# Gating each half of the scan branch's projection at once, and adding it to the other branch in DRAM by adding transfers

## The chip, the cores and the metric

The kernel runs on one core of one Trainium2 chip. Its engines are TensorE (PE in the profile; its weight loads are a row of their own, PEld), VectorE (DVE), ScalarE (ACT), GpSimd (POOL) and SyncE (SP). Each works through its own instructions in order and waits on the others by semaphores. Transfers between DRAM and on-chip memory are issued by an engine (rows marked SPq and ACTq: issued by SP or by ACT) and carried out by 16 DMA engines. The metric is the device time of one execution, in microseconds (us).

## The reference, cut to what matters

One residual block for 512 positions of width 2048. Two branches are computed from one input projection, a retention branch (`y_r`, width 2048) and a scan branch (`y_s`, width 4096). What the change touches is how they are merged:

```python
y_s = rmsnorm((y_s * silu(z)), ssd_norm_w)
p_r = einsum('bse,ed->bsd', y_r, w_br_ret)      # 2048 -> 2048
p_s = einsum('bse,ed->bsd', y_s, w_br_ssd)      # 4096 -> 2048
merged = sigmoid(gate_r) * p_r + sigmoid(gate_s) * p_s
x = x + einsum('bsd,de->bse', merged, w_out)    # 2048 -> 2048
return rmsnorm(x, norm_f_w)
```

The inner dimension of `p_s` is twice that of `p_r`, and the kernel computes it in two halves. The scale of `y_s`'s norm is one number per position, so the kernel applies it after the projection, together with the gate.

## The kernel before, in words

All activations are kept transposed: channels on the 128 partitions, 512 positions along a row. A projection has three parts:

- `load_operands` (L192) brings 8 operand tiles `r` of 256 rows into on-chip memory and prepares them (`first_half`, L168 to L175, on DVE and ACT). `second_halves` (L177 to L185) prepares the other operands (`b`) that the units 1 to 6 need.
- `unit` (L249) computes 256 output rows. There are 8 units in a projection of 2048 outputs. Units 0 and 7 are plain (96 matmuls of 512 columns), units 1 to 6 use a scheme of seven products (168 matmuls of 256 columns). For each of 8 inner steps the weights are loaded by SP (`wf`, L227; 3 buffers), combined by DVE (L230 to L233), split into a high part `whi` (ACT, L148) and a low part `wlo` (DVE, L149), and multiplied by PE (L213 to L215). At the end ACT and DVE collect the sums into a tile `o` (2 buffers, L261 to L270), whose two halves are the 128 x 512 outputs `x`.
- The loop around it does something with each `x`.

Four projections stand behind each other at the end, and this text names them so:

- the **retention projection** (L696 to L704): each output is multiplied by its gate `gr_d` and stored to `m_d` in DRAM;
- the **first scan half** (L709 to L715), over rows 0 to 2047 of `ys_d`: each output is stored as it is to `ps_d`;
- the **second scan half** (L716 to L731), over rows 2048 to 4095: for each output SP loads the partial result `ps_d`, the gate `gs_d` and the other branch `m_d`; POOL multiplies the gate by the norm's scale `R2` (L726); DVE adds the partial result (L727), multiplies by the gate (L728) and adds the other branch (L729); ACT stores to `mm_d` (L731). For unit 7 the result stays on chip as the last operand tile;
- the **output projection** (from L732): its operands are the seven tiles of `mm_d` and the last one.

The tiles that the loops around `unit` load are called `f` and share 4 buffers (L689 to L694). The program is put in order by a scheduler that simulates it, and weight loads have a higher priority than the rest. So SP's queue is one row of weight loads (L227), loads of `f` (L693) and of operands (L197), in an order fixed when the program is built; one that waits holds up all that stand behind it.

## Time and profile before

| what | value |
|---|---|
| time, median of 3 runs (lowest to highest) | 2768.85 us (2766.91 to 2770.41) |
| the profiled execution: its own time / its span | 2769.07 us / 2767.2 us |
| TensorE busy | 2699.1 us (98% of the span) |
| VectorE busy | 2371.0 us (86%) |
| ScalarE busy | 1343.0 us (49%) |
| GpSimd busy | 175.2 us (6%) |
| DMA | 362.46 MB, mean 131 GB/s |

The own time of the profiled execution lies 1.87 us above its span and 0.22 us above the median of the runs. TensorE is the engine that sets the length nearly everywhere; the four projections at the end take up the last fifth, from about 2050 us. Times below are microseconds from the start of the span.

### The profile page before, as it was taken

The page shows a single profiled execution, that of the slowest core. Times are in us where ns is not written, and L with a number is a line of the kernel's source. Part 1 is how long each engine was busy: PE and PEld are TensorE (multiplying, and loading weights), DVE is VectorE, ACT ScalarE, POOL GpSimd, SP SyncE. Part 2 cuts the span into 40 slices and gives each one's busy share as a digit, 9 for nine tenths or more (in the row PEclk, how much of TensorE's full clock was granted, in tenths as well). Part 3 has the DMA queues.
Part 4 walks back from the last instruction along what each step waited for, and adds up shares of the span by engine and source line. Part 5 has one row for each costly group of instructions (what it writes and reads, how often), then busy time and mean ns, then how long its engine had stood idle before and what let it go on. Part 6 is the DMA issues. An engine that isn't in the chain of part 4 may idle for free.

```text
span 2767.2 us, 51984 instructions
## 1 busy us (share of the span) xinstructions
PE 2699.1 (98%) x20448; PEld 2567.6 (93%) x20448; DVE 2371.0 (86%) x3799; ACT 1343.0 (49%) x1923; POOL 175.2 (6%) x130
## 2 busy tenths in 40 slices
PE   6999999999999999999999999999999999999998
PEld 3799999999999999999999999999999989899898
DVE  8788888888878898898989888898889798898997
ACT  4334333343336555566565556556564353433453
POOL 0000000000000100000000000000000000011221
PEclk8999999999999999999999999999999999999999
DMA  4233333333333434343443434344464544557634
GB/s 141 77 96 92 115 100 107 96 100 103 104 112 107 141 108 127 121 129 121 128 142 120 136 108 128 116 132 126 131 200 144 192 155 141 179 169 230 203 123 138
DMA packets 339766, 362.46 MB, mean 131 GB/s; under 512 B 25152, under 2 KB 297792, under 8 KB 339520
## 3 DMA queue, kind: packets, MB, share of 16 engines
q1 hardware_dynamic: 319136, 325.05, 38.2%
q10 hardware_dynamic: 20384, 34.09, 3.3%
q8 instruction: 160, 2.62, 0.4%
q14 instruction: 86, 0.70, 0.1%
HBM read 321.56 MB, written 37.49 MB: 130 GB/s over the span
## 4 chain that ended last, share of the span: by engine, by line
PE 75%; DVE 11%; DMA 8%; issue 3%; ACT 1%; SPq 1%; POOL 0%; DVEq 0%; ACTq 0%; POOLq 0%
PE pb L215 21%; PE pb L214 21%; PE pb L213 20%; DVE wlo L149 3%; DMA wf<-in_w_in_dram 3%; DMA wf<-in_w_br_ssd_dram 2%; PE att L215 2%; PE att L214 2%; PE att L213 2%; PE att L549 1%; PE att L534 1%; DVE wf L230 1%; PE att L666 1%; PE pb L118 1%; PE att L670 1%
## 5 line engine op out<-in xcount | busy, mean ns | idle before, releaser
L148 ACT CAST whi<-wf 128x896 fp32r<-128x896 f32 (+1 forms) x968 | 818.5, 884 | 925.8 <-PE pb L214 390.0
L149 DVE TENSOR_TENSOR wlo<-wf,whi 128x896 fp32r<-128x896 f32 (+1 forms) x968 | 989.9, 1034 | 64.4 <-ACT whi L148 33.3
L213 PE MATMUL pb<-a,whi 128*128 128x256 f32 (+1 forms) x3328 | 1001.8, 304 | 13.7 <-ACT a L118 9.4
L214 PE MATMUL pb<-a,whi 128*128 128x256 f32 (+1 forms) x3328 | 1002.4, 302 | 8.7 <-DVE a L118 8.7
L215 PE MATMUL pb<-a,wlo 128*128 128x256 f32 (+1 forms) x3328 | 999.6, 302 | 5.9 <-DVE wlo L149 5.9
L213 PEld LDWEIGHTS pb<-a,whi 128*128 128x128 f32 x3328 | 636.7, 192 | 41.5 <-ACT a L118 13.3
L214 PEld LDWEIGHTS pb<-a,whi 128*128 128x128 f32 x3328 | 639.1, 192 | 33.9 <-DVE a L118 12.8
L215 PEld LDWEIGHTS pb<-a,wlo 128*128 128x128 f32 x3328 | 637.9, 192 | 29.9 <-DVE wlo L149 7.7
L213 PE MATMUL pb<-b,whi 128*128 128x256 f32 x2112 | 599.6, 284 | 0.0
L215 PE MATMUL pb<-b,wlo 128*128 128x256 f32 x2112 | 598.8, 284 | 0.0
L214 PE MATMUL pb<-b,whi 128*128 128x256 f32 x2112 | 598.0, 284 | 0.0
L230 DVE TENSOR_TENSOR wf<-wf 128x512 f32<-128x512 f32 x400 | 286.2, 715 | 185.3 <-DMA wf<-in_w_in_dram 138.7
L214 PEld LDWEIGHTS pb<-b,whi 128*128 128x128 f32 x2112 | 405.4, 192 | 0.1
L215 PEld LDWEIGHTS pb<-b,wlo 128*128 128x128 f32 x2112 | 405.3, 192 | 0.2
L213 PEld LDWEIGHTS pb<-b,whi 128*128 128x128 f32 x2112 | 405.4, 192 | 0.0
L233 DVE TENSOR_TENSOR wf<-wf 128x256 f32<-128x256 f32 x400 | 175.5, 439 | 3.4
L232 DVE TENSOR_TENSOR wf<-wf 128x256 f32<-128x256 f32 x400 | 174.5, 436 | 3.6
L215 PE MATMUL att<-a,wlo 128*128 128x256 f32 (+1 forms) x480 | 144.6, 306 | 5.3 <-DVE wlo L149 5.3
L213 PE MATMUL att<-a,whi 128*128 128x256 f32 (+1 forms) x480 | 145.5, 305 | 0.0
L214 PE MATMUL att<-a,whi 128*128 128x256 f32 (+1 forms) x480 | 145.3, 305 | 0.0
L215 PEld LDWEIGHTS att<-a,wlo 128*128 128x128 f32 x480 | 91.0, 192 | 10.3 <-DVE wlo L149 6.5
L659 ACT ACTIVATE L<-L,sst 128x128 f32<-128x128 f32 x256 | 78.5, 390 | 35.8 <-DMA L<-A_d 35.8
(221 smaller groups left out, 2736.6 us busy)
## 6 DMA issues: line engine op xcount, KB each, us to landing
wf<-in_w_in_dram SPq DMA_DIRECT2D x640, 256.0 KB, 3.1
wf<-in_w_br_ssd_dram SPq DMA_DIRECT2D x128, 256.0 KB, 3.4
wf<-in_w_out_dram SPq DMA_DIRECT2D x72, 256.0 KB, 3.2
wf<-in_w_in_dram SPq DMA_DIRECT2D x128, 128.0 KB, 2.6
L<-A_d SPq DMA_DIRECT2D x32, 512.0 KB, 3.7
wf<-in_w_br_ret_dram SPq DMA_DIRECT2D x64, 256.0 KB, 3.4
ys_d<-B ACTq DMA_DIRECT2D x32, 256.0 KB, 2.1
r<-ys_d SPq DMA_DIRECT2D x16, 512.0 KB, 6.1
```

The lines of the kernel that those rows point to most:

```text
L118: ins = getattr(self.engine, name)(*args, **kw).ins
L148: ACT.copy(dst_hi, src)
L149: DVE.tensor_tensor(dst_lo, src, dst_hi.bitcast(F32), op=ALU.subtract)
L213: PE.matmul(o, wh, xh, start=b not in started, stop=False, skip_group_check=True)
L214: PE.matmul(o, wh, xl, start=False, stop=False, skip_group_check=True)
L215: PE.matmul(o, wl, xh, start=False, stop=(k == NP - 1), skip_group_check=True)
L230: DVE.tensor_tensor(f2[:, :, 4:6, :], f2[:, :, 1:3, :], f2[:, :, 0:1, :].to_broadcast([P, 2, 2, P]), op=ALU.subtract)
L232: DVE.tensor_tensor(f2[:, :, 0, :], f2[:, :, 2, :], f2[:, :, 4, :], op=ALU.add)
L233: DVE.tensor_tensor(f2[:, :, 6, :], f2[:, :, 3, :], f2[:, :, 0, :], op=ALU.subtract)
L534: PE.matmul(ps[:, :n], k[:, i, sb * P:(sb + 1) * P], q[:, i, sb * P:], start=(i == 0), stop=(i == 1))
L549: PE.matmul(ps[:, :DK], pt[sb][:, (lb - sb) * P:(lb - sb + 1) * P], v[:, sb, :], start=(sb == 0), stop=(sb == lb))
L659: ACT.activation(L[:, i, c, :], L[:, i, c, :], AF.Relu, scale=-1.0, bias=At[:, c, h0 + i:h0 + i + 1])
```

## The change

Each half of the scan branch's projection is now gated as soon as it is computed. In the first scan half SP loads the gate, POOL multiplies it by the norm's scale, ACT stores the scaled gate to a new DRAM array `ss_d`, DVE multiplies the output by it in place (in `o`), and POOL issues a transfer from `o` to `m_d` that adds to what is there. The second scan half loads the scaled gate, multiplies, and adds to `m_d` in the same way; for unit 7 it loads `m_d` and adds on chip. The output projection reads its operands from `m_d`. The arrays `ps_d` and `mm_d` are gone. The text calls the new transfers "adding transfers". Line numbers after the change are up to 3 higher from here on, and 1 lower ahead of it.

```diff
-    ps_d = dp.tile([D, T], F32, name="ps_d")
+    ss_d = dp.tile([D, T], F32, name="ss_d")
     m_d = dp.tile([D, T], F32, name="m_d")
-    mm_d = dp.tile([D, T], F32, name="mm_d")
...
             for e, x in enumerate(unit([w_s[:D, i * 256:(i + 1) * 256]], i % 2, i in PLAIN2)):
                 j = 2 * i + e
-                ACT.dma_start(out=ps_d[j * P:(j + 1) * P, :], in_=x)
+                s = rtile(gs_d, j)
+                POOL.tensor_tensor(s, s, R2, op=ALU.mult)
+                ACT.dma_start(out=ss_d[j * P:(j + 1) * P, :], in_=s)
+                DVE.tensor_tensor(x, x, s, op=ALU.mult)
+                POOL.dma_start(out=m_d[j * P:(j + 1) * P, :], in_=x, accum_op=ALU.add)
         load_operands(ys_d[D:, :])
...
             for e, x in enumerate(unit([w_s[D:, i * 256:(i + 1) * 256]], i % 2, i in PLAIN2)):
                 j = 2 * i + e
-                p = rtile(ps_d, j, last[:, e, :] if i == NP - 1 else None)
-                s, m = rtile(gs_d, j), rtile(m_d, j)
-                POOL.tensor_tensor(s, s, R2, op=ALU.mult)
-                DVE.tensor_tensor(p, p, x, op=ALU.add)
-                DVE.tensor_tensor(p, p, s, op=ALU.mult)
-                DVE.tensor_tensor(p, p, m, op=ALU.add)
+                s = rtile(ss_d, j)
                 if i < NP - 1:
-                    ACT.dma_start(out=mm_d[j * P:(j + 1) * P, :], in_=p)
-        load_operands(mm_d, NP - 1)
+                    DVE.tensor_tensor(x, x, s, op=ALU.mult)
+                    POOL.dma_start(out=m_d[j * P:(j + 1) * P, :], in_=x, accum_op=ALU.add)
+                else:
+                    m = rtile(m_d, j)
+                    DVE.tensor_tensor(s, s, x, op=ALU.mult)
+                    DVE.tensor_tensor(last[:, e, :], s, m, op=ALU.add)
+        load_operands(m_d, NP - 1)
```

SP's queue in the middle of the second scan half, before (`f` tiles are the small loads, `wf` the weights):

```order
L693 DMA f_27273<-gs_d_85 128x512
L693 DMA f_27275<-m_d_87 128x512
L693 DMA f_27282<-ps_d_86 128x512
L227 DMA wf_27553<-in_w_br_ssd_dram 128x2x256 x2
L227 DMA wf_27609<-in_w_br_ssd_dram 128x2x256 x2
L693 DMA f_27284<-gs_d_85 128x512
L227 DMA wf_27665<-in_w_br_ssd_dram 128x2x256 x2
L693 DMA f_27286<-m_d_87 128x512
L693 DMA f_27527<-ps_d_86 128x512
L693 DMA f_27529<-gs_d_85 128x512
L227 DMA wf_27700<-in_w_br_ssd_dram 128x2x256 x2
L693 DMA f_27531<-m_d_87 128x512
```

So the queue before alternates between the two kinds. The same queue at the same place after the change:

```order
L692 DMA f_27578<-ss_d_86 128x512
L692 DMA f_27582<-ss_d_86 128x512
L227 DMA wf_27460<-in_w_br_ssd_dram 128x2x256 x2
L227 DMA wf_27495<-in_w_br_ssd_dram 128x2x256 x2
L227 DMA wf_27590<-in_w_br_ssd_dram 128x2x256 x2
L227 DMA wf_27646<-in_w_br_ssd_dram 128x2x256 x2
L692 DMA f_27820<-ss_d_86 128x512
L692 DMA f_27824<-ss_d_86 128x512
```

Before, six loads of `f` for a unit stand singly between its eight weight loads; after, two stand together ahead of eight weight loads.

POOL's queue at the start of the first scan half after the change (there was nothing there before; `m_d` rows are the adding transfers, two for a unit):

```order
L715 TENSOR_TENSOR f_25160<-f_25160,R1_81 128x512
L715 TENSOR_TENSOR f_25166<-f_25166,R1_81 128x512
L715 TENSOR_TENSOR f_25448<-f_25448,R1_81 128x512
L715 TENSOR_TENSOR f_25454<-f_25454,R1_81 128x512
L718 DMA m_d_87<-o_25153 128x512 x2
L715 TENSOR_TENSOR f_25694<-f_25694,R1_81 128x512
L715 TENSOR_TENSOR f_25700<-f_25700,R1_81 128x512
L718 DMA m_d_87<-o_25442 128x512 x2
```

The 16 products by `R2` have moved from the second scan half to here, and run two units ahead of the outputs that they gate.

DVE's queue at the end of the second scan half after the change: the last two outputs of unit 6 are gated (L729), and the load of that tile back from `m_d` is first used in the row L173 of `r6`:

```order
L729 TENSOR_TENSOR o_28540<-o_28540,f_28546 128x512
L729 TENSOR_TENSOR o_28540<-o_28540,f_28550 128x512
L149 TENSOR_TENSOR wlo_28656<-wf_28652,whi_28655 128x512
L175 TENSOR_TENSOR a0_28720<-r0_28718,a0_28720 128x1024
L149 TENSOR_TENSOR wlo_28660<-wf_28652,whi_28659 128x512
L175 TENSOR_TENSOR a1_28726<-r1_28724,a1_28726 128x1024
L149 TENSOR_TENSOR wlo_28788<-wf_28784,whi_28787 128x512
L175 TENSOR_TENSOR a2_28732<-r2_28730,a2_28732 128x1024
L173 TENSOR_TENSOR r6_28754<-r6_28754 128x256
L149 TENSOR_TENSOR wlo_28804<-wf_28784,whi_28803 128x512
```

Six rows stand between the gating and that first use; the rows of unit 7's collecting (L262 to L734) and of the preparing of `b` tiles for the output projection (L181, L182) come behind it.

## Rows read from the trace of the kernel before

**Rows 1.** The page: busy us, share of the span, instructions, by engine.

```profile
PE 2699.1 (98%) x20448; PEld 2567.6 (93%) x20448; DVE 2371.0 (86%) x3799; ACT 1343.0 (49%) x1923; POOL 175.2 (6%) x130
```

**Rows 2.** Busy time by stretch: retention, first and second scan half, output projection's start.

```profile
core 0: us, PE busy (x) PEld busy (x) DVE busy (x) ACT busy (x) POOL busy (x), PEclk, DMA share, GB/s
2070.00:2230.00 160.00, 160.00 (x1182) 153.28 (x1181) 137.83 (x215) 67.86 (x89) 0.00 (x0) 1.00 0.53 175
2234.03:2401.05 167.02, 165.92 (x1204) 157.49 (x1202) 138.27 (x213) 69.81 (x91) 1.57 (x1) 1.00 0.49 158
2401.05:2577.15 176.10, 168.09 (x1201) 158.95 (x1200) 159.34 (x241) 68.23 (x90) 24.43 (x14) 0.99 0.62 199
2577.15:2632.00 54.85, 50.43 (x304) 45.48 (x303) 52.30 (x84) 26.77 (x35) 16.67 (x3) 0.94 0.50 168
```

**Rows 3.** Order of time, PE: start, us, what, [idle before <- releaser].

```profile
2538.65 0.48 PE L215 MATMUL pb<-a,wlo 128*128 128x256 f32 x1 [2.73 <-DVE wlo L149]
```

**Rows 4.** Chain of waits ahead of that row: start, us, what.

```profile
2524.44 5.89 DMA mm_d<-f
...
2530.35 0.32 SPq L693
...
2531.20 5.68 DMA wf<-in_w_br_ssd_dram
...
2536.90 0.04 DVE wf L230
```

**Rows 5.** What SP's queue waited for, second scan half: us, times, longest.

```profile
SPq L227 <- DVE wlo L149: 58.9, 20, 7.9
SPq L693 <- DMA mm_d<-f: 24.7, 9, 5.6
SPq L693 <- DVE f L728: 13.7, 6, 2.9
```

**Rows 6.** The same, retention projection.

```profile
SPq L693 <- DMA m_d<-f: 16.1, 8, 4.7
```

**Rows 7.** DVE in the second scan half: count | busy, mean ns | idle before.

```profile
L175 DVE TENSOR_TENSOR a<-r,a 128x1024 fp32r<-128x1024 f32 x9 | 10.9, 1216 | 0.0
...
L149 DVE TENSOR_TENSOR wlo<-wf,whi 128x512 fp32r<-128x512 f32 x16 | 10.7, 681 | 0.0
L729 DVE TENSOR_TENSOR f<-f 128x512 f32<-128x512 f32 x14 | 10.0, 718 | 0.1
L728 DVE TENSOR_TENSOR f<-f 128x512 f32<-128x512 f32 x14 | 9.6, 684 | 6.9 <-POOL f L726 6.9
L727 DVE TENSOR_TENSOR f<-f,o 128x512 f32<-128x512 f32 x14 | 9.2, 681 | 0.8 <-DMA f<-ps_d 0.8
```

**Rows 8.** Order of time: a product on POOL, and DVE instructions without and beside one.

```profile
2459.73 0.41 DVE L232 TENSOR_TENSOR wf<-wf 128x256 f32<-128x256 f32 x1
...
2483.62 1.81 POOL L726 TENSOR_TENSOR f<-f,R 128x512 f32<-128x512 f32 x1 [13.98 <-DMA f<-gs_d]
...
2484.18 1.52 DVE L232 TENSOR_TENSOR wf<-wf 128x256 f32<-128x256 f32 x1
```

**Rows 9.** Order of time, DVE, from the second scan half to the output projection.

```profile
2560.14 0.69 DVE L270 TENSOR_TENSOR o<-pb,o 128x512 f32<-128x512 f32 x1
...
2574.75 0.68 DVE L729 TENSOR_TENSOR f<-f 128x512 f32<-128x512 f32 x1
...
2585.54 0.41 DVE L173 TENSOR_TENSOR r<-r 128x256 f32<-128x256 f32 x1
...
2593.78 1.29 DVE L181 TENSOR_TENSOR xo<-r 128x512 f32<-128x512 f32 x2
```

**Rows 10.** Order of time, SP at the same place.

```profile
2579.94 0.43 SPq L197 DMA_DIRECT2D r<-mm_d  x1
```

**Rows 11.** DMA issues: count, KB each, median us to landing.

```profile
mm_d<-f ACTq DMA_DIRECT2D x14, 256.0 KB, 4.6
r<-mm_d SPq DMA_DIRECT2D x7, 512.0 KB, 4.6
```

**Rows 12.** Order of time, POOL in the output projection.

```profile
2616.38 14.61 POOL L753 TENSOR_TENSOR R<-R,o 128x512 f32<-128x512 f32 x1 [35.63 <-ACT R L750]
```

## The prediction

> **What bounds the kernel now.** I read the page first, for the engine that sets the length. The reader is to see that PE is busy for 98% of the span while DVE has 86% and POOL 6% [rows 1]: less work on DVE or in DRAM is worth nothing by itself, only where PE stands still.
>
> Next the busy times cut by stretch, each cut laid at the first matmul of a projection, so that the three stretches in the middle can be compared. They show where PE stands still. In the retention projection it is busy for 160.00 of 160.00 us. The first scan half takes 167.02 us with 1.1 us idle. The second scan half, with the same matmuls (1201 records against 1204), takes 176.10 us: 9.1 us more. At the start of the output projection PE is busy for 50.43 of 54.85 us, and the granted clock averages 0.94, so a part of it runs at the lower of the two levels: 4.4 us idle and some 0.06 x 54.85 = 3.3 us by the clock, 7.7 us together [rows 2]. These are the 17 us to be had at most; nothing else in these stretches waits.
>
> Then the order of time and the chain of waits, for who makes PE wait. In the second scan half it is always `wlo`, the low part of the weights from DVE; the longest stop is 2.73 us at 2538.65 [rows 3]. The chain ahead of it reads: an `f` buffer is given back only when the store to `mm_d` has landed (5.89 us); SP's next load of `f` waits for that; behind it in SP's queue stands a weight load, which lands 5.68 us after its issue; only then can DVE combine the weights [rows 4]. Last the queue's own waits, for how often: SP waited 24.7 us in 9 pieces for the `mm_d` stores and 13.7 us in 6 pieces for L728 [rows 5]. In the retention projection it waited for `m_d` stores too, 16.1 us [rows 6], and PE lost nothing. So a wait of this kind becomes a loss when DVE has no slack: DVE was busy for 137.83 of 160 us there, and for 159.34 of 176.10 here [rows 2].
>
> **The change part by part.**
>
> *Second scan half.* The 14 each of L727 to L729 cost 9.2, 9.6 and 10.0 us, and DVE waited 6.9 us for POOL's product ahead of L728 [rows 7]. One multiplication of about 0.68 us for each of 14 outputs stays, 9.5 us: DVE's 159.34 us fall by 28.8 - 9.5 = 19.3 to 140.0, and the wait goes. That is the first half's load (138.27), nearly. SP has two loads of `f` for a unit where it had six, and no buffer waits for a store any more: `f` is free when DVE has read it. What is held longer is `o`, until the adding transfer has landed; `o` has two buffers and a unit takes some 20 us (a stretch of 8 units takes 167), so a transfer has nearly 40 us, and hides. I expect the first half's length: **-9 us**. The bounds are 0, if the adding transfers themselves make the weight loads late, and -10.2, if the idle 1.1 us goes as well.
>
> *First scan half.* DVE gets 16 multiplications, 16 x 0.68 = 10.9 us, and POOL's 16 products come here. They are not free for DVE: beside the product at 2483.62 an instruction of 0.41 us took 1.52 [rows 8]. So each product costs DVE between nothing (if DVE is idle) and 1.1 us, 0 to 17.6 us together, and DVE's load becomes 149 to 167 us of 167. The Trainium skill says the same (SBUF — State Buffer, Who interferes with whom): a DVE instruction with two SBUF inputs and a GpSimd instruction that reads SBUF take a shared port from each other for a whole instruction. It also forbids the hope that the product is hidden because POOL is idle; by it the sum would tend to the upper end, which is the second rival below.
>
> The DMA engines get 16 gate loads and 16 adding transfers more: 32 x 0.26 = 8.4 MB in 167 us, 50 GB/s on top of 158 [rows 2], what the second half had (199). ACT's queue gets 16 stores of scaled gates that wait for POOL; behind the first ones stand casts of the weights. Products run two units ahead of their use, so after the start nobody waits for them. The bounds are -1.1 us (it becomes like the retention projection, which had a gate and a store for each output and lost nothing) and +9.1 (it becomes like the second half). It gets the second half's load without its SP chain; I take a third, **+3 us**.
>
> *Into the output projection.* Before, the last tile went from L729 (ended at 2575.4) by a store and a load (issued at 2579.94, when the store had landed) to L173 at 2585.54, and DVE came to L181, the first `b` tile, at 2593.78, 16.6 us after the first matmul at 2577.15 [rows 9, 10]. PE then waits for `b` tiles. After: unit 6 is collected at 2560.8 (L270), and two multiplications are done at 2562.2. Let T be the time from there until both adding transfers have landed. The load takes 5.6 us as before, so DVE reaches L173 of that tile at 2567.8 + T. From there to L181 stand 23 instructions of 0.41 to 1.22 us [rows 7, 9], 17.1 us as recorded and about 15.3 with their overlap of some 0.08 us: L181 comes at 2583.1 + T. It is earlier than before if T is under 10.7 us. T is not in the trace. From below it is a plain store, 4.6 us [rows 11] plus its issue, 5 us. From above each of two issues takes POOL as long as its longest instruction, 14.61 us in a stretch in which DVE was never idle [rows 12]: 2 x 14.6 + 4.6 = 33.8 us. I take 8 us: one issue at the 1.8 us of a product, and a landing between one store and a store with a load (4.6 and 9.2 us), and L181 comes 2.7 us earlier: **-2.5 us**.
>
> The Trainium skill has a price for a transfer from this queue (DMA: Bandwidth & Descriptors, Anatomy of one DMA): about 2.0 us plus the bytes at 436 GB/s, an estimate of 2.6 us for 256 KB. By that T would be about 4 us and the first rival would come true; no run here shows such a transfer so far.
>
> *What brings nothing:* the number of transfers. 16 stores, 48 loads and 14 stores become 34 loads, 16 stores and 30 adding transfers, each of which reads its target too.
>
> **Sum.** -9 + 3 - 2.5 = -8.5 us. Against the profiled execution's own 2769.07 us (its span of 2767.2 and 1.87 around it; the median of the runs is 0.22 lower) that is 2760.5 us.
>
> **Rivals.**
>
> *The way into the output projection becomes clean* (T near 5 us, and the first half loses nothing): -9 - 6 + 0 = -15, 2754 us. For it: the retention projection has nearly this form and loses nothing. Against it: DVE is full at the start of the output projection (52.30 of 54.85 us) and most of that work stays.
>
> *The stop moves to the first scan half*: DVE at 167 of 167 us there, PE stops as it did in the second, +9.1: -9 + 9.1 - 2.5 = -2.4, 2766.7 us. For it: the 1.1 us beside each product. Against it: SP's chain by way of stores, which ended the longest stop, is not there.
>
> *The adding transfers are late at the end (slower).* POOL's issue is held up as L753 was. In the middle `o`'s two buffers hide it. At the end, SP's load of the last tile waits for it, and behind that load stand weight loads; DVE's L173 waits, and behind it everything for the output projection. Each us of T above 10.7 costs one. With both issues at 14.6 us T is 33.8, +23: -9 + 3 + 23 = +17, 2786 us. It is slower by over 0.2% from a T of about 22 us. For it: a POOL instruction did take 14.61 us. Against it: the 14 products in the second half took 24.43 us together, 1.7 each, while DVE was busy for nine tenths of the time. The Trainium skill speaks against it as well (SBUF — State Buffer, the box on DVE blocking DMA): descriptors are held up by DVE's two-port modes, which copies use and these instructions do not; no run here shows it.
>
> **How the numbers follow.** The forecast has 40%, the clean way 22%, the moved stop 25%, the late transfers 13%. A measurement of this kernel can tell about 0.2% (5.5 us) from no change: faster is below 2763.3, slower above 2774.4. Forecast and clean way are faster, 62%; the moved stop is no change, 25%; the late transfers are slower, 13%. The range runs from 2753, just under the clean way, to 2772, past the moved stop (2767) and a T of some 20 us; beyond it lie most of the late transfers and a little of the clean way. The forecast's own range is 2757 to 2764.
>
> **What would show it.** In the changed profile, cut at the same matmuls: the second scan half near 167 us, with no wait of SP for a store; the first near 170, with DVE over 155 us busy; POOL's products at 1.3 to 2.4 us. L181 should come some 14 us after the output projection's first matmul. The forecast is wrong if the second half stays above 172 us (then the SP chain was not what made DVE late), if the first grows past 175, or if L173 of the last tile comes later than 2580 on the clock of before.

## The result and the profile after

The changed kernel is slower, not faster: 2775.56 us (median of 8 runs, 2769.97 to 2777.13) against 2766.84 us of the kernel before on the same chip. The ratio is 1.0029, 95% interval 1.0018 to 1.0040. Its profiled execution took 2776.12 us (span 2774.3); forecast were 2760.5, at most 2772.

First the page's engines, which answer to [rows 1], and the busy times by stretch, cut at the same matmuls and with the same columns as [rows 2].

```profile
PE 2700.9 (97%) x20448; PEld 2568.1 (93%) x20448; DVE 2363.4 (85%) x3785; ACT 1342.9 (48%) x1923; POOL 210.2 (8%) x160
```

```profile
2070.00:2230.00 160.00, 160.00 (x1181) 153.25 (x1181) 138.55 (x218) 67.60 (x89) 0.00 (x0) 1.00 0.53 175
2234.32:2408.86 174.54, 168.99 (x1204) 159.93 (x1202) 151.46 (x224) 68.39 (x88) 40.78 (x30) 0.98 0.66 193
2408.86:2580.89 172.03, 166.08 (x1201) 157.06 (x1200) 137.19 (x213) 70.52 (x94) 14.05 (x16) 1.00 0.61 167
2580.89:2636.00 55.11, 48.39 (x276) 42.26 (x275) 51.64 (x83) 24.57 (x33) 13.96 (x1) 0.94 0.45 149
```

DVE has 7.6 us less to do and the kernel is longer. The table compares the stretches with the forecast; the last one runs from the output projection's first matmul to the end of the span.

| stretch | before | after | change | forecast |
|---|---|---|---|---|
| ahead of the first scan half | 2234.03 | 2234.32 | +0.3 | 0 |
| first scan half | 167.02 | 174.54 | +7.5 | +3 |
| second scan half | 176.10 | 172.03 | -4.1 | -9 |
| output projection to the end | 190.05 | 193.41 | +3.4 | -2.5 |
| span | 2767.2 | 2774.3 | +7.1 | -8.5 |

All three steps came out worse. The order of time shows PE's four longest stops (each ends at the time given; in brackets how long PE was idle, and for whom):

```profile
2262.23 0.80 PE L215 MATMUL att<-a,wlo 128*128 128x256 f32 x2 [4.14 <-DVE wlo L149]
...
2425.91 0.50 PE L214 MATMUL pb<-a,whi 128*128 128x512 f32 x1 [1.71 <-DVE a L175]
...
2436.07 0.51 PE L215 MATMUL att<-a,wlo 128*128 128x256 f32 x2 [1.81 <-DVE wlo L149]
...
2599.05 1.22 PE L213 MATMUL pb<-a,whi 128*128 128x512 f32 x2 [2.79 <-ACT a L174]
```

They lie at the starts of the two halves and of the output projection, not in the middle of a stretch as before [rows 3]. For the first, POOL and DVE ahead of it, in order of time:

```profile
2254.76 6.47 POOL L715 TENSOR_TENSOR f<-f,R 128x512 f32<-128x512 f32 x4 [201.34 <-DMA f<-gs_d]
```

```profile
2253.52 0.41 DVE L233 TENSOR_TENSOR wf<-wf 128x256 f32<-128x256 f32 x1
...
2255.22 1.51 DVE L182 TENSOR_TENSOR g<-r,g 128x256 f32<-128x256 f32 x1
2256.66 1.51 DVE L233 TENSOR_TENSOR wf<-wf 128x256 f32<-128x256 f32 x1
2258.09 2.02 DVE L149 TENSOR_TENSOR b<-g,b 128x768 fp32r<-128x768 f32 x1
2260.03 2.15 DVE L149 TENSOR_TENSOR wlo<-wf,whi 128x896 fp32r<-128x896 f32 x1
2262.10 0.41 DVE L232 TENSOR_TENSOR wf<-wf 128x256 f32<-128x256 f32 x1
2262.44 1.08 DVE L149 TENSOR_TENSOR wlo<-wf,whi 128x896 fp32r<-128x896 f32 x1
```

Four products in a row lengthen the four DVE instructions beside them by some 1.1 us each (L233 0.41 without, 1.51 beside; L149 for wlo 1.08 and 2.15): 4.4 us, and PE stops 4.14 us for the last of them. It is the price of [rows 8], paid four times at a place where DVE, which is preparing the `b` tiles, has no slack.

Late in that stop the granted clock fell to the lower of its two levels (2.4 and 1.2 GHz) and stayed there for 6.9 us (columns as in [rows 2]):

```profile
2260.90:2267.80 6.90, 5.57 (x26) 5.57 (x27) 6.90 (x10) 1.67 (x2) 0.33 (x1) 0.51 0.36 126
```

There a matmul of 256 columns starts every 0.21 us, behind it every 0.12. So the first half's +7.5 us are some 4.4 us more of PE's idle time (174.54 - 168.99 against 167.02 - 165.92) and up to 3.4 us (0.49 x 6.90) of clock.

What SP waited for in the second half shows that the chain by way of stores [rows 4, 5] has indeed gone; the second line is now the short wait for the adding transfers, ahead of the loads of operand tiles:

```profile
SPq L227 <- DVE wlo L149: 77.0, 22, 8.5
...
SPq L197 <- DMA m_d<-o: 5.6, 2, 4.5
```

DVE's own waits of that half grew instead: weights that land late, 18.6 us in 12 pieces, where the kernel before lost 8.6 us in 8:

```profile
DVE wf L230 <- DMA wf<-in_w_br_ssd_dram: 18.6, 12, 3.2
DVE r L173 <- DMA r<-m_d: 8.6, 4, 6.1
```

Most of these waits cost PE nothing: from 2451 to 2546 it was busy for 93.98 of 95.00 us. Of this half's stops two lie at its start and one ahead of unit 7, where DVE had just waited twice for weights:

```profile
2451.00:2546.00 95.00, 93.98 (x780) 93.61 (x780) 76.05 (x118) 34.24 (x44) 7.08 (x8) 1.00 0.55 147
```

```profile
2537.93 0.69 DVE L230 TENSOR_TENSOR wf<-wf 128x512 f32<-128x512 f32 x1 [3.05 <-DMA wf<-in_w_br_ssd_dram]
...
2543.38 0.69 DVE L230 TENSOR_TENSOR wf<-wf 128x512 f32<-128x512 f32 x1 [1.47 <-DMA wf<-in_w_br_ssd_dram]
```

```profile
2546.64 0.39 PE L215 MATMUL pb<-a,wlo 128*128 128x256 f32 x1 [1.66 <-DVE wlo L149]
```

Last the way into the output projection, in order of time on DVE, which answers to [rows 9]:

```profile
2560.38 0.42 DVE L173 TENSOR_TENSOR r<-r 128x256 f32<-128x256 f32 x1 [6.11 <-DMA r<-m_d]
2563.22 0.42 DVE L173 TENSOR_TENSOR r<-r 128x256 f32<-128x256 f32 x1 [1.81 <-DMA r<-m_d]
...
2567.78 0.68 DVE L270 TENSOR_TENSOR o<-pb,o 128x512 f32<-128x512 f32 x1
...
2569.32 1.28 DVE L729 TENSOR_TENSOR o<-o,f 128x512 f32<-128x512 f32 x2
...
2582.15 0.43 DVE L173 TENSOR_TENSOR r<-r 128x256 f32<-128x256 f32 x1 [6.33 <-DMA r<-m_d]
...
2597.84 1.29 DVE L181 TENSOR_TENSOR xo<-r 128x512 f32<-128x512 f32 x2
```

DVE's queue is in order: it stands for operand tiles of units up to 5 (L173, 6.11 and 1.81 us) ahead of collecting unit 6 (L270), and then 6.33 us for unit 6's tile. SP's load of that tile (which answers to [rows 10]) came 8.0 us after the end of the two L729:

```profile
2578.57 0.37 SPq L197 DMA_DIRECT2D r<-m_d  x1
```

The issues, with the median time to landing, against [rows 11]:

```profile
m_d<-o POOLq DMA_DIRECT2D x30, 256.0 KB, 7.0
r<-m_d SPq DMA_DIRECT2D x7, 512.0 KB, 8.4
```

### The profile page after: what moved, and what is told of

Its sections match the earlier page's. It is cut to its first block, busy times and chain, and to the rows that moved or that the text cites. A ratio compares the mean times of both kernels' runs of the same rounds, so it can differ in the third digit from the quotient of the medians.

```text
span 2774.3 us, 52018 instructions
## 1 busy us (share of the span) xinstructions
PE 2700.9 (97%) x20448; PEld 2568.1 (93%) x20448; DVE 2363.4 (85%) x3785; ACT 1342.9 (48%) x1923; POOL 210.2 (8%) x160
## 4 chain that ended last, share of the span: by engine, by line
PE 81%; DVE 10%; DMA 4%; issue 3%; ACT 1%; SPq 0%; DVEq 0%; POOL 0%; ACTq 0%
PE pb L215 22%; PE pb L214 22%; PE pb L213 22%; PE att L215 3%; PE att L214 3%; PE att L213 3%; DVE wlo L149 3%; DMA wf<-in_w_in_dram 2%; PE att L548 1%; PE att L533 1%; PE att L665 1%; DMA wf<-in_w_br_ssd_dram 1%; PE pb L118 1%; DVE wf L230 1%; PE att L669 1%
## 5 line engine op out<-in xcount | busy, mean ns | idle before, releaser
L149 DVE TENSOR_TENSOR wlo<-wf,whi 128x896 fp32r<-128x896 f32 (+1 forms) x968 | 990.0, 1035 | 68.6 <-ACT whi L148 36.0
L230 DVE TENSOR_TENSOR wf<-wf 128x512 f32<-128x512 f32 x400 | 287.0, 718 | 191.2 <-DMA wf<-in_w_in_dram 139.0
L233 DVE TENSOR_TENSOR wf<-wf 128x256 f32<-128x256 f32 x400 | 179.0, 449 | 3.5
L637 POOL TENSOR_TENSOR xl<-xd,sst 128x384 f32<-128x384 f32 x32 | 35.1, 1098 | 845.2 <-DVE xd L634 786.3
```

The lines of the kernel that those rows point to most:

```text
L149: DVE.tensor_tensor(dst_lo, src, dst_hi.bitcast(F32), op=ALU.subtract)
L230: DVE.tensor_tensor(f2[:, :, 4:6, :], f2[:, :, 1:3, :], f2[:, :, 0:1, :].to_broadcast([P, 2, 2, P]), op=ALU.subtract)
L233: DVE.tensor_tensor(f2[:, :, 6, :], f2[:, :, 3, :], f2[:, :, 0, :], op=ALU.subtract)
L637: POOL.tensor_tensor(xl, xd[:, :TB - 1], tail[:, :TB - 1, hs, None].to_broadcast([P, TB - 1, 2, 64]), op=ALU.mult)
```

## The experiments

Theories: A, POOL's products beside DVE make the first half long; B, the adding transfers make loads late (W: since loads of `m_d` must wait until they have landed; L: since they load the DMA engines); C, SP's loads of gates wait for a buffer, and weights stand behind them. Each run was timed in five rounds beside the kernel before on the same chip; the ratio is to that. Stages are from one profiled execution each. They vary: six kernels with the changed first half whole had 174.5, 172.8, 172.5, 171.2, 171.1 and 171.5 us there, so one or two microseconds in one stage say nothing. The last column also holds the clock: granted 0.96 on average in the changed kernel, 0.94 in adding_second and 0.98 in second_plain_store, some 4 us either way. PE's idle time in that stretch separates the kernels that are one edit away from the changed one more clearly: 18.3 to 20.2 us where unit 6's operand tile comes through an adding transfer (the changed kernel and as_changed, no_scaling, adding_second, scaled_early, first_as_before), 14.4 to 15.8 us in the other six.

| kernel | ratio (95%) | first half | second half | to the end |
|---|---|---|---|---|
| before | 1 | 167.0 | 176.1 | 190.1 |
| changed | 1.0029 (1.0018 to 1.0040) | 174.5 | 172.0 | 193.4 |
| as_changed | 1.0023 (1.0014 to 1.0032) | 172.8 | 171.9 | 193.6 |
| no_scaling | 1.0011 (1.0002 to 1.0020) | 167.9 | 173.0 | 193.2 |
| plain_transfers | 0.9981 (0.9971 to 0.9992) | 169.4 | 167.1 | 188.0 |
| adding_first | 0.9992 (0.9983 to 1.0001) | 171.1 | 169.3 | 188.6 |
| adding_second | 1.0005 (0.9995 to 1.0016) | 170.7 | 168.1 | 194.8 |
| plain_twice | 0.9981 (0.9970 to 0.9991) | 170.0 | 166.5 | 187.0 |
| adding_elsewhere | 0.9999 (0.9990 to 1.0008) | 171.5 | 172.5 | 186.1 |
| unit6_kept | 1.0005 (0.9997 to 1.0014) | 171.2 | 173.7 | 187.6 |
| first_as_before | 0.9987 (0.9978 to 0.9996) | 165.9 | 171.4 | 191.2 |
| second_plain_store | 1.0007 (0.9998 to 1.0016) | 172.5 | 172.8 | 184.1 |
| scaled_early | 1.0057 (1.0044 to 1.0070) | 169.3 | 172.2 | 192.7 |
| fb_unit6 | 0.9978 (0.9969 to 0.9987) | 166.0 | 166.4 | 192.2 |
| fb_early_unit6 | 1.0009 (0.9999 to 1.0018) | 166.1 | 167.2 | 189.9 |
| before_kept | 0.9989 (0.9980 to 0.9998) | 165.4 | 173.4 | 189.2 |
| hybrid | 0.9966 (0.9952 to 0.9979) | 166.5 | 169.1 | 187.4 |

### The products

```diff
                 s = rtile(gs_d, j)
-                POOL.tensor_tensor(s, s, R2, op=ALU.mult)
```

> Leaves out POOL's 16 products with R2 in the first scan half (the gates go unscaled into both halves, so the normalisation of the scan branch is missing from the output); loads, stores, multiplications and adding transfers stay. Theory A (the four products in a row at the start of the first half lengthen DVE's instructions beside them, 1.1 us each, and PE stops for that): the first half falls from 174.5 us by 4 to 5, to about 170, and the whole from 2775.6 to about 2771; the later stages do not change. Theory B (the adding transfers and the 16 loads more are what makes weights and tiles late): first half 173 to 175, whole 2774 to 2777. Theory C (SP's loads of gates wait for the multiplication that frees their buffer, and weights stand behind them): first half 173 to 175 as well, since that wait stays.

The first half fell to 167.9, 6.7 us less, with no stop at its start; the other stages stayed. A holds; B and C had said 173 to 175. Up to 3.4 of the 6.7 us are the clock, granted at 1.00 in this half here. (Leaving the products out also changes the order that the scheduler makes, so part of it may be order.) The products were then moved ahead, into the retention projection, where DVE has slack:

```diff
+            if i == 1:
...             # R2 is computed here
+            for j in SCALED[i]:   # 2 or 3 gates a unit, units 1 to 6
+                s = rtile(gs_d, j)
+                POOL.tensor_tensor(s, s, R2, op=ALU.mult)
+                ACT.dma_start(out=ss_d[j * P:(j + 1) * P, :], in_=s)
...             # the first scan half
-                s = rtile(gs_d, j)
-                POOL.tensor_tensor(s, s, R2, op=ALU.mult)
-                ACT.dma_start(out=ss_d[j * P:(j + 1) * P, :], in_=s)
+                s = rtile(ss_d, j)
```

> As the changed kernel, but R2 is computed after unit 1 of the retention projection, and the gates are loaded, multiplied by R2 on POOL and stored to ss_d during units 1 to 6 of that projection; the first scan half only loads the scaled gates. Same work in all, no product in the first half. Theory A (the products beside DVE at the first half's start): the first half loses its stops of 2257 to 2283, 174.5 to about 168 us, as without the scaling; the retention projection has DVE at 138 of 160 us and takes the products without loss; the stop between the halves (4.6 us) and the start of the output projection (193.4 to the end) stay, since the adding transfers do. Whole about 5 less than the changed kernel, 1.001 of before. Rival: what is moved costs the retention projection as much (SP gets two or three loads more for a unit, and f has four buffers), and the whole stays at 1.003.

The rival won, and worse than it said. The first half did fall to 169.3, but PE stopped in the retention projection, which took 176.0 us, before 164.5. What SP waited for there, and PE's stop:

```profile
SPq L693 <- DMA ss_d<-f: 26.0, 10, 4.2
SPq L693 <- DMA m_d<-f: 12.8, 10, 3.2
```

```profile
2189.83 0.58 PE L216 MATMUL att<-a,wlo 128*128 128x256 f32 x1 [4.62 <-DVE wlo L150]
```

A gate's buffer is given back when its store has landed; SP stands for that, 26.0 us in 10 pieces, with weights behind. This is the chain of [rows 4] made anew in the stage that had been free of it.

### Adding transfers against plain stores

The cleanest pair: only the addition is left out, and every engine has the same instructions in the same order.

```diff
-                POOL.dma_start(out=m_d[j * P:(j + 1) * P, :], in_=x, accum_op=ALU.add)
+                POOL.dma_start(out=m_d[j * P:(j + 1) * P, :], in_=x)
```

> The 30 adding transfers become plain stores from the same queue and of the same tiles to the same places (the sum over the branches is not formed: each store replaces what stood there). Everything else stays. Theory B (reading the target as well costs DMA time and makes other loads late): landings of these stores fall from 7.0 us to some 4.6, those of r<-m_d from 8.4 towards 5, the first half gets 2 to 4 us shorter and the stretch from the output projection's start to the end falls from 193.4 to about 190; whole about 2769. Theory A (the products beside DVE): the first half stays at 174 to 175, the whole loses at most the 3.4 us of the output projection's start, 2772 to 2776. Theory C: as A.

It gave more than B said: 0.9981 against 1.0029, 0.0048 or 13 us (12 against as_changed), from all three stages. The second half is at 167.1, the length forecast for it. The two queue rows (packets, MB, share of 16 engines), of the changed kernel and of this one:

```profile
q0 software_dynamic: 4320, 7.87, 1.8%
```

```profile
q0 software_dynamic: 2400, 7.87, 0.7%
```

The same 30 tiles take 1.8 times the packets (the data goes in packets of 2 KB, with plain stores of 4 KB) and some 2.6 times the engines' time. The Trainium skill (Collectives: The Full Stack, "The bandwidth ceiling: the fold count and why AG ≠ RS ≠ AR") says of the ring ReduceScatter that it is slower not because the addition costs but because it needs two source reads, which puts twice the reading traffic on the queue for a byte delivered; the 2.6 here is more than that, and no run here measures the reading of the target by itself. One place of both kernels, in the second half just after the transfers of unit 2, shows what it does to others: the issues from there with their landings, and DVE's next combining of weights, changed kernel first:

```profile
wf<-in_w_br_ssd_dram SPq DMA_DIRECT2D x4, 256.0 KB, 4.8
f<-ss_d SPq DMA_DIRECT2D x2, 256.0 KB, 4.4
m_d<-o POOLq DMA_DIRECT2D x2, 256.0 KB, 6.8
```

```profile
2494.64 0.69 DVE L230 TENSOR_TENSOR wf<-wf 128x512 f32<-128x512 f32 x1 [3.23 <-DMA wf<-in_w_br_ssd_dram]
```

```profile
wf<-in_w_br_ssd_dram SPq DMA_DIRECT2D x4, 256.0 KB, 3.9
f<-ss_d SPq DMA_DIRECT2D x2, 256.0 KB, 4.3
m_d<-o POOLq DMA_DIRECT2D x2, 256.0 KB, 4.3
```

```profile
2482.05 0.69 DVE L230 TENSOR_TENSOR wf<-wf 128x512 f32<-128x512 f32 x1 [0.91 <-DMA wf<-in_w_br_ssd_dram]
```

Behind adding transfers the weights land in 4.8 us for 3.9 (the gates in 4.4 for 4.3, no difference), and DVE stands 3.23 us for 0.91. PE lost nothing at this place; the same delay ahead of unit 7 ended in the stop of 1.66 us at 2546.64, which is not there with plain stores. Over the half DVE's wait for weights is 10.7 us with plain stores and 18.6 with adding ones. The median landing over the whole half (3.3 and 3.4 us) hides it. It is the weight loads issued 1 to 3 us behind the nearest issue of these transfers that are late: 6.55 us in the median (10 loads) for 4.55 (11 loads) with plain stores. Those issued 1 to 4 us ahead of one take 3.1 us in both.

Which half's transfers cost? The same edit in one half only, again in the same order of instructions; first in the second half alone (adding_first), then in the first alone (adding_second), and the changed kernel once more:

```diff
             (second half, L730)
-                    POOL.dma_start(out=m_d[...], in_=x, accum_op=ALU.add)
+                    POOL.dma_start(out=m_d[...], in_=x)
```

> Adding transfers only in the first scan half; those of the second are plain stores to the same places (the second half's part replaces the sum there). Order of instructions on every engine as in the changed kernel. All plain gave 0.9981 of before with 169.4, 167.1 and 188.0 us (first half, second half, from the output projection's start to the end), all adding 1.0029 with 174.5, 172.0 and 193.4. If the cost arises where adding transfers run beside the operand loads of the next stage: first half 171 to 174, second half 170 to 171 (its stop of 3.5 us at the start comes back, the one of 1.7 us ahead of unit 7 does not), 188 to the end; whole 1.000 to 1.001. If it is the second half's transfers that cost most: 0.9985.

```diff
             (first half, L718)
-                POOL.dma_start(out=m_d[...], in_=x, accum_op=ALU.add)
+                POOL.dma_start(out=m_d[...], in_=x)
```

> The reverse: plain stores from POOL's queue in the first half (they replace the other branch's part), adding transfers in the second; order of instructions as in the changed kernel. By the first reading: first half 169 to 170, second half 168 to 169 without the stop at its start, 192 to 193.5 to the end, since unit 6 is collected late and goes by an adding transfer; whole 1.000 to 1.001. If the wait at the end builds up from the start of the second half: 188 to 190 to the end and 0.9985 to 0.9995.

> The changed kernel again, beside the two with half of the adding transfers, for how much the lengths of its stages vary between executions: the first half was 174.5 us in its profile, while three kernels with the same work there had 171.2 to 172.5. Its instructions in the first half say 4.1 us of stop at 2257 for four products in a row. If that is the rule: 173 to 175, whole 1.003 of before. If it was one slow execution: 171 to 172.5, second half 172, 193 to the end, whole 1.002 to 1.003.

The first reading holds, more or less. With adding transfers in the first half only, the stop for `a` L175 at the second half's start is there (1.71 us, and 1.72 for wlo; second half 169.3) and the end is as with plain stores (188.6). With them in the second half only, that stop is gone (168.1) and the end has the loss (194.8, with PE idle for 18.3 us; 19.2 in the changed kernel, 15.2 with plain stores). In as_changed the 4.1 us stop did not come again; the first half was 172.8, with its clock granted at 1.00, the same 5.6 us of idle time in all and stops of 0.5 to 1.4 us between 2272 and 2292. Six other kernels with the products stop at that place for 1.6 to 2.8 us. So the first half's loss is about 4 to 7.5 us, and one stop of 4 us is not the rule.

The wait for the landing, or the load? Adding into an array that nobody reads keeps the load and takes away the wait:

```diff
-                POOL.dma_start(out=m_d[...], in_=x, accum_op=ALU.add)
+                POOL.dma_start(out=yr_d[...], in_=x, accum_op=ALU.add)
```

> The 30 adding transfers add into yr_d, which nothing reads any more, and m_d keeps the other branch alone (the scan branch is missing from the sum for units 0 to 6). The number, size and kind of the transfers and all waits on DVE and POOL stay; what goes is that loads of m_d wait for them. Theory W (what costs is the wait: loads of operand tiles start only when adding transfers have landed): the time falls as with plain stores, the start of the output projection from 193.4 to 188 us to the end, the whole to 0.998 to 0.999 of before. Theory L (what costs is the load on the DMA engines, 1.8% of their time for 30 adding transfers against 0.7% for 30 plain ones): halves stay at 171 to 174.5 and 172 to 173.5, 191 to 193 to the end, whole 1.002 to 1.003 of before.

Both, in different places. The second half stays at 172.5 and DVE's wait for weights at 18.2 us: there it is the load (L). To the end it is 186.1 us: there it is the wait (W), though more of it than the landing. Unit 6's tile now does not depend on unit 6 at all, and SP issues its load 19.7 us ahead of the output projection's first matmul, in the changed kernel 2.3 us ahead. Two plain stores for each adding transfer:

```diff
-                POOL.dma_start(out=m_d[...], in_=x, accum_op=ALU.add)
+                POOL.dma_start(out=m_d[...], in_=x)
+                POOL.dma_start(out=yr_d[...], in_=x)
```

> Each adding transfer becomes two plain stores from the same queue, one to m_d, one to yr_d (no sum is formed): about the DMA time of an adding transfer (some 1.4% of the engines against 1.8), 60 issues on POOL, and the landing of a plain store (5.2 us with one). Theory L (load on the DMA engines): most of what one plain store instead of an adding transfer gave (the changed kernel at 1.0029, one plain store at 0.9981) is lost again, 1.001 to 1.003. Theory W (the wait for the landing, or what only an adding transfer does): it stays near one plain store, 0.998 to 0.9995.

It stayed at 0.9981, with 1.5% of the engines' time against 1.8. That speaks against a mere sum of engine time; but this kernel's order of instructions differs from the changed one's, so it does not settle it. Why an adding transfer holds up its neighbours more than its share of time says is open.

### The way into the output projection, and better kernels

Unit 6 finished on chip, as unit 7 is (here and in the four kernels with it, `last = raw_tile(i)` stands behind the unit's matmuls for the last two units):

```diff
-                if i < NP - 1:
+                if i < NP - 2:
                     DVE.tensor_tensor(x, x, s, op=ALU.mult)
...
-        load_operands(m_d, NP - 1)
+        load_operands(m_d, NP - 2)
```

> As the changed kernel, but unit 6 of the second scan half is finished as unit 7 is: DVE multiplies, adds the loaded m and writes the operand tile itself, so that tile does not go by an adding transfer and a load (8.0 us until both transfers have landed, 3.6 for the load; DVE stood 6.33 us for it). Two additions more on DVE (1.4 us), two adding transfers and one load less. If that way is what delays the start of the output projection: 193.4 falls to 187 to 189 us to the end. If DVE is late there because it stands for the operand tiles of units 0 to 5 ahead of collecting unit 6 (6.1 us at 2560.38): 191 to 193. The halves stay at 174.5 and 172. Whole 0.998 to 0.999 of the changed kernel by the first (1.001 of before), 1.0025 of before by the second.

187.6 us to the end: the way of unit 6 through DRAM is what costs there. The rival's observation is true and not enough: unit 6 is still collected late (9.1 us after unit 7's first matmul, 8.7 in the changed kernel), yet L181 now comes 11.6 us after the output projection's first matmul instead of 17.0.

The change undone in the first half, where `ss_d` then holds the partial projection:

```diff
-                s = rtile(gs_d, j)
-                POOL.tensor_tensor(s, s, R2, op=ALU.mult)
-                ACT.dma_start(out=ss_d[...], in_=s)
-                DVE.tensor_tensor(x, x, s, op=ALU.mult)
-                POOL.dma_start(out=m_d[...], in_=x, accum_op=ALU.add)
+                ACT.dma_start(out=ss_d[...], in_=x)
...
-                s = rtile(ss_d, j)
+                p, s = rtile(ss_d, j), rtile(gs_d, j)
+                POOL.tensor_tensor(s, s, R2, op=ALU.mult)
+                DVE.tensor_tensor(x, x, p, op=ALU.add)
```

> Undoes the change in the first scan half only: there the partial projection is stored plainly, as before; in the second half the partial projection and the gate are loaded, POOL scales the gate there, DVE adds and multiplies, and the result goes to the other branch by adding transfers for units 0 to 6. So the second half has 14 additions more than after (9.5 us of DVE) and the 16 products, but SP waits for no store of mm_d. All theories: first half back to 167 us (7.5 less). If what made the second half slow before was SP's wait for the landing of mm_d, it stays at 172 us or less although DVE has 150 us of work; if it was DVE's load, it goes to 174 to 176. The start of the output projection has the adding transfers as after: if they are what costs there, it stays at 193 us to the end. Whole: 2768 by the first reading, 2770 to 2772 by the second.

The first half is back at 165.9, and this kernel beats both. Its second half takes 171.4 us with DVE busy for 150.18: of the two readings SP's wait, not DVE's work. fb_unit6 below says so more clearly, with DVE busy for 150.7 us and 166.4 us in all.

Undone in the second half:

```diff
-                s = rtile(ss_d, j)
+                s, m = rtile(ss_d, j), rtile(m_d, j)
+                DVE.tensor_tensor(s, s, x, op=ALU.mult)
                 if i < NP - 1:
-                    DVE.tensor_tensor(x, x, s, op=ALU.mult)
-                    POOL.dma_start(out=m_d[...], in_=x, accum_op=ALU.add)
+                    DVE.tensor_tensor(s, s, m, op=ALU.add)
+                    ACT.dma_start(out=mm_d[...], in_=s)
```

> Keeps the change in the first scan half (scaled gates, adding transfers into m_d) and undoes it in the second: there m_d is loaded for every output, DVE multiplies and adds, and ACT stores the sum plainly to mm_d, from which the output projection's tiles are loaded. 14 more additions on DVE (9.5 us) and 14 more loads on SP than after, and buffers wait for stores again. First half unchanged, 174.5. Second half: 175 to 176 if the wait of SP for these stores was what mattered, 172 if only DVE's work did (DVE then has about 147 us of it, against 159 before). From the output projection's start to the end: 190 as before if the adding transfers are what made unit 6 late there (theory B), 193 if something else did. Whole 2774 to 2776 by the first of each.

The way to the end, 184.1 us, is the shortest of all, without an adding transfer there: the reading by B, and more. PE's idle time in it, 14.4 us, is near that with plain stores (15.2); the rest is the clock, granted at 0.98 on average here and at 0.95 there. The second half, 172.8, lies between the two readings, with 16.1 us of waiting for stores of `mm_d`, and says nothing clear: 3.4 us of it are the clock (0.98), and 1.7 us of its 3.9 us of idle time are the stop at its start.

Combinations of these edits: first_as_before with unit6_kept; the same with the gates scaled in the retention projection; and the kernel before with unit 6 kept (`p` loaded into the operand tile, as for unit 7):

> First half as before (plain store of the partial projection), second half with the partial projection and gate loaded, POOL's product, DVE adding and multiplying, adding transfers for units 0 to 5 only; units 6 and 7 are added by DVE straight into the operand tiles. Against the version with adding transfers for units 0 to 6 (0.9987 of before; halves 165.9 and 171.4, 191.2 from the output projection's start to the end): if the way of unit 6 by DRAM matters, 187 to the end and 0.997 of before; if the tiles of units 0 to 5 do, 190 to 191 and 0.9985.

> As the one with the first half as before and unit 6 kept, and the gates scaled by POOL during the retention projection (stored to ss_d, loaded in the second half), so neither half has products. The second half of the version with products there had stops at 2473 and 2517 (4.7 us), where a product stood beside the subtraction for wlo (2.17 us for 1.08). If the product is the cause, the second half falls from 171.4 to 167 to 168 us; if the late weight loads behind SP's f loads are, it stays at 171. The first half stays at 166 if it has nothing left that stops it. Whole 0.995 to 0.996 of before by the first, 0.997 to 0.9985 by the second.

```diff
-                p = rtile(ps_d, j, last[:, e, :] if i == NP - 1 else None)
+                p = rtile(ps_d, j, last[:, e, :] if i >= NP - 2 else None)
...
-                if i < NP - 1:
+                if i < NP - 2:
                     ACT.dma_start(out=mm_d[...], in_=p)
```

> The kernel before, without adding transfers, with one edit: unit 6 of the second half is finished into its operand tile by DVE, not by a store to mm_d and a load. It tells whether the gain of the version with the first half as before and unit 6 kept (0.9978) comes from keeping unit 6 or from adding transfers in the second half. If from keeping unit 6: second half 174 to 176 as before, 186 to 188 to the end, 0.998 of before. If the adding transfers of units 0 to 5 are what relieves the second half (no load of m, one addition less for each output, no buffer that waits for a store): second half 174 to 176 and 188 to 190 to the end, 0.999 to 1.000 of before.

fb_unit6 came to 0.9978, but by its second half (166.4), not by its end (192.2), so neither reading of its text is right. fb_early_unit6 lost its halves, 166.1 and 167.2, to the stop in the retention projection (4.99 us) that scaled_early has. Its second half agrees with its first reading, but fb_unit6 has 166.4 with the products, so it does not show that they were the cause. before_kept gave 0.9989 with a second half of 173.4, where SP again waited 23.1 us for stores: its text's second reading. The last combination gates units 6 and 7 as the change does, the others as first_as_before:

```diff
+                if i < NP - 2:
+                    ACT.dma_start(out=ps_d[j * P:(j + 1) * P, :], in_=x)
+                    continue
                 s = rtile(gs_d, j)       # units 6 and 7 as in the change
...
-                s = rtile(ss_d, j)
-                if i < NP - 1:
+                if i < NP - 2:
+                    p, s = rtile(ps_d, j), rtile(gs_d, j)
+                    POOL.tensor_tensor(s, s, R2, op=ALU.mult)
+                    DVE.tensor_tensor(x, x, p, op=ALU.add)
                     DVE.tensor_tensor(x, x, s, op=ALU.mult)
                     POOL.dma_start(out=m_d[...], in_=x, accum_op=ALU.add)
                 else:
-                    m = rtile(m_d, j)
+                    s, m = rtile(ss_d, j), rtile(m_d, j)
...
```

> Units 0 to 5 as in the version with the first half as before and unit 6 kept (plain store of the partial projection; second half: add, gate, adding transfer), units 6 and 7 gated in the first half with adding transfers, as the changed kernel does, and finished by DVE in the second with one multiplication and one addition each. So the way into the output projection has 4 DVE additions and 4 loads less than in that version (0.9978 of before, 192.2 us from the output projection's start to the end). If DVE's load is what makes it late there: 188 to 190 us to the end and 0.996 to 0.997 of before. If the adding transfers of the last units of the first half cost the crossing into the second (4.6 us in the changed kernel at 2423 to 2434), that comes back: second half 170 instead of 166.4, and the whole 0.998 to 0.999.

It has the lowest ratio, 0.9966 (0.9952 to 0.9979): 9 us faster than before and 16 to 17 than the change. Its interval overlaps that of fb_unit6, so which of the two is faster is not shown. The end is at 187.4, near its first reading, with a part of the loss at the crossing (169.1). Its stretches (columns as in [rows 2]):

```profile
2230.20:2396.72 166.52, 166.32 (x1204) 157.59 (x1202) 141.59 (x214) 69.96 (x92) 19.59 (x7) 1.00 0.51 168
2396.72:2565.78 169.06, 165.88 (x1201) 157.30 (x1200) 156.44 (x231) 67.49 (x89) 37.92 (x26) 1.00 0.65 187
2565.78:2620.89 55.11, 53.26 (x327) 48.43 (x326) 52.74 (x86) 28.32 (x38) 21.42 (x1) 0.94 0.50 171
```

DVE is busy for 156.44 of 169.06 us in the second half, 19 us more than in the changed kernel, and PE loses less (3.2 us idle, 5.95 there): what DVE has to do there matters less than when its weights come.

## Why the prediction was wrong

**Second scan half, forecast -9, measured -4.1.** The step that SP's chain by way of stores made it long was right. PE's idle time in this half is 8.0 us before and 7.3 in before_kept, where SP waits 23 to 25 us for stores; it is 1.4 in fb_unit6 and 3.2 in the last kernel, where no load of `f` waits for a store, though DVE is busy for 150.7 and 156.4 us there. With plain stores of the same tiles the half takes 167.1 us, the 167 forecast. The step that failed is "a transfer has nearly 40 us, and hides". The transfer hides; what it does to the loads beside it does not. The text had this as its bound ("0, if the adding transfers themselves make the weight loads late") and then took the other end. Its own sign of being wrong (above 172 us "the SP chain was not what made DVE late") would have misled: the chain was gone, and what the addition costs came in its place. Mis-sized: 167 us, measured 172.0, of which 4.9 go with the addition alone. And of the 4.1 us gained only 2.1 are idle time of PE (8.01 to 5.95). Another 1.7 are the clock, for which the forecast had no term in this half: behind the stop at 2538.65 [rows 3] it was granted at 0.50 for 3.4 us, and in the changed kernel's second half at 1.00 throughout.

```profile
2538.80:2542.20 3.40, 3.40 (x17) 3.40 (x18) 3.40 (x6) 0.00 (x0) 0.93 (x1) 0.50 0.59 221
```

**First scan half, forecast +3, measured +7.5 (+5.8 in the second execution).** The prediction said "after the start nobody waits for them", and the start is where it was lost: four products beside DVE, 1.1 us each. The size of one was known [rows 8]; that four come in a row at the start stood in POOL's queue and was not priced there. Nor was the clock, up to 3.4 us behind that stop, which the second execution did not have. Without products it is 167.9. About 2 us of the rest go with the addition: 169.4 and 170.7 us in the two kernels with plain stores there, 172.3 on average in the six with adding ones.

**Into the output projection, forecast -2.5, measured +3.4.** T was taken as 8 us and measured 8.0 (7.3 with plain stores, so the addition is not what makes it long). The tile reached DVE 3.6 us after its load was issued, not 5.6. The step that failed is the start of the chain: unit 6 was assumed to be collected when it was before, 4.8 us after unit 7's first matmul; it was collected after 8.7, since DVE stood for loads of other operand tiles ahead of it (8.6 us in four pieces). Its two multiplications ended 11.5 us after that matmul, with plain stores 6.3. So L181 came 17.0 us after the output projection's first matmul, not 14. The other 3 us are put down to PE's own order, which was not looked at: in the output projection's first unit the last operand tile is now first used by the 67th of 96 matmuls, before by the 81st. That is 14 matmuls of 0.227 us, 3.2 us earlier, and PE stopped 2.79 us for it at 2599.05. No run changes this order alone.

**What brings nothing: the number of transfers.** The number did not matter where it was tried: twice as many plain stores gave 0.9981 as well, if in another order of instructions. The kind did: the sentence saw that an adding transfer "reads its target too" and put that at nothing, and the addition in the 30 transfers is worth 12 to 13 us.

**The rivals.** The moved stop came nearest: its place was right for the first half and its price near (+9.1, measured +7.5 and +5.8), though DVE was busy for 151 us there and not for 167; but it kept -9 for the second. The slower rival's price did not come: two issues took POOL 1.75 us (0.9 each, not 14.6) and the chain ends as forecast after them; the kernel is slower for other reasons. No rival held what an adding transfer does to its neighbours; only the lower bound of the second half did.

## What to carry to other kernels

A transfer that is hidden itself can still cost by what it delays: price it at the loads that are issued just behind it, above all those at the head of the next stage, and compare adding and plain transfers in the same order of instructions. Move work to where the receiving engine has slack at that moment, not on the average of the stage, and ask again which buffers it holds until a store lands. At the last tile of a stage, what needs no way through DRAM should not take one.

## What the runs showed of the hardware

An adding transfer of 256 KB landed 7.0 us after its issue in the median, a plain store from the same queue 5.2; its issue took POOL 0.88 us against 0.54, and its data went in packets of 2 KB, not 4. Weight loads issued 1 to 3 us behind one landed in 6.55 us, behind a plain store in 4.55 (medians of 10 and 11 loads). Four DVE instructions of three shapes (0.41, 0.94 and 1.08 us) were each lengthened by the same 1.1 us beside a product on POOL, whatever their own length. The median landing of all loads of that class (3.3 and 3.4 us) did not show a delay for which DVE waited 8 us longer in one stage. Late in PE's stop of 4.14 us the granted clock fell to 0.51 for 6.9 us, behind the stop of 2.73 us in the kernel before to 0.50 for 3.4 us.
